# Decay matrices of all eight chunks scanned ahead of the chunks and kept in DRAM

## The chip, the cores and the metric

The kernel runs on one core of a Trainium2 chip. The core has a matrix engine (TensorE, PE in the profile; PEld is its weight load), a vector engine (VectorE, DVE), an engine for activations (ScalarE, ACT), a general one (GpSimd, POOL) and SyncE (SP), whose queue issues every DMA of this kernel. Each engine works through its own instructions in order and waits for semaphores of the others. The metric is the device time of one execution in microseconds (us). Before the change it is 1239.85 us, the median of three runs (1236.53 to 1240.24).

## The reference

One decoder layer in float32: 1024 tokens of width 1024, with 16 learned meta tokens ahead. A normalised input goes through one projection, three groups of heads read it (stick-breaking attention, a Mamba-2 recurrence called SSD, and HGRN2), and their outputs go through an output projection and a squared-ReLU MLP. The change is in the SSD group, which works in chunks of 128 tokens:

```python
acum = jnp.cumsum(a_c, axis=1)
seg = acum[:, :, None, :] - acum[:, None, :, :]
decay = masked_decay(seg, causal[None, :, :, None])          # exp(seg) where s <= t, else 0
cb = jnp.repeat(jnp.einsum('btgn,bsgn->btsg', c_c, b_c), rep, axis=-1)
y_diag = jnp.einsum('btsh,bshp->bthp', cb * decay, x_c)
```

For each chunk and each of 8 heads this needs a 128x128 matrix of decays: the product of the factors exp(a) of all tokens after s up to t. These matrices depend on the step sizes `dt` alone, not on the state that is carried from chunk to chunk.

## The kernel before

**Stages.** The kernel is one long instruction stream per engine. First come the normalised input and its transposes, then the attention with the other projections as fillers between its products, then a short stretch that projects the HGRN2 inputs and computes the meta tokens' states, then eight chunks of 128 tokens (SSD, HGRN2 and the output projection of the chunk before), then the MLP. Matrix products are done with operands split into a high and a low part, three products for one (`split_scaled`, `split`).

**The factors.** `decays()` computes exp(dt * a) for all tokens, transposes it to 8 rows (one per head) and stores it as `dr_g` (8 x 1040). In `chunk(c)` one DMA loads the chunk's 128 factors of all 8 heads, repeated on all 128 partitions, into `dec` (128 x 8 x 128, 512 KB). Two DVE scans (`tensor_tensor_scan` with multiply and add, 128 x 512 each, four heads each) turn it into the decay matrices: the second operand, `ident4`, is four identity matrices, so partition s starts its running product at t = s. The scans stand after the first and the second of seven HGRN2 levels (`LEVELS`, `hg_level`), behind that level's `copy_predicated` on DVE. Levels 3 and 4 multiply `dec` by C·B, and at the chunk's end eight products of `dec` with the inputs give `y_diag`.

**The end of the attention.** The attention's 32 heads (8 query tiles, 4 heads) each need a running product `kp` and a `sg` tile. Between the products of the last heads (`values`, VGAP, SGAP, HGAP) the PE works on fillers (`fill`, `all_fillers`): last of all `z_tile(i)`, i = 1 to 8, called z1 to z8 below. Each z tile is 24 products into one of two `mf` banks; ACT takes the sigmoid of the bank into an `igt` tile, DVE multiplies the bank by it, and a DMA stores the tile to `dr_z`. The bank is free for the next tile but one after the DVE multiply. At the same time `load_wi` loads the eight parts of the next projection's weight by DMA (`st<-in_w_in_dram`) and splits each part on ACT and DVE into `g` tiles. After z8 `ig_all` uses those weights: its first tile, `ig0` (the 16 meta tokens), needs all eight parts.

**What sets the order.** PE's order is that of the code (`queue`, L112). On the other engines the tile framework's scheduler chooses the order from its own estimate, within dependencies and the hints of `behind` (L80). Every queue, SP's too, is then worked through in order: a DMA that waits for a semaphore holds up all DMAs after it. All DMAs of the kernel go through SP's one queue. SBUF tiles come from rings of buffers by tag; `k4` has four buffers (128 x 1072) and serves the attention heads' `kp` and `sg`, then `xb` and `dec` of each chunk. In the profile all vector, scalar and DMA instructions carry the helper's line L96, all products L119 and all transposes L122, so tiles name the work.

Of the kernel before, what the change touches and what calls it, by code (L numbers as in the profile page):

```python
# [13 lines left out]
ALU = mybir.AluOpType  # L14

P = 128
D = 1024
KC = D // P
SEQ = 1024
NT = SEQ // P  # L20
NM = 16
L = SEQ + NM
G3 = L + 16
K4 = L + 48
# [44 lines left out]
def tile_hybrid_block(  # L69
# [8 lines left out]
    fixed, last, lastkv, lastcp, urgent = [False], [None], [None], [None], [None]  # L78

    def behind(i, j):  # L80

        tc.add_manual_dep(i.ins, j.ins.name,
                          mybir.DependencyInfo(mybir.DependencyClass.NoSync, mybir.DependencyReason.DATA),
                          reason="issue order")
# [19 lines left out]
    V, A, G, SY = (Pinned(e) for e in (nc.vector, nc.scalar, nc.gpsimd, nc.sync))  # L104
# [28 lines left out]
    def sb(shape, tag, dt=F32):  # L133
        if tag in ring:
            r = ring[tag]
            r[3] += 1
            at = r[0] + r[3] % r[1] * r[2]
            return cx[:, at:at + shape[0]]
        cnt[0] += 1
        return pool.tile([P] + list(shape), dt, tag=tag, bufs=BUFS[tag], name=f"{tag}_{cnt[0]}")  # L140

    def const(shape, name, dt=F32):
        return pool.tile([P] + list(shape), dt, tag=name, bufs=1, name=name)

    def ps(tag):
        cnt[0] += 1
        return psp.tile([P, 512], F32, tag=tag, bufs=PBUFS[tag], name=f"{tag}_{cnt[0]}")

    def dram(shape, name):
        return drp.tile(list(shape), F32, name=name)  # L150
# [9 lines left out]
    dr_ig = dram([SEQ, 512], "dr_ig")  # L160
    dr_o = dram([SEQ, 256], "dr_o")
    dr_g = dram([8, L], "dr_g")
    dr_h = dram([SEQ, D], "dr_h")
    dr_s = [dram([NQ, P, 512], f"dr_s{i}") for i in range(7)]
    dr_m = dram([NQ, P, 512], "dr_m")
# [96 lines left out]
    ident4 = const([512], "ident4", U8)  # L262
# [519 lines left out]
    dec = decays()  # L782
# [40 lines left out]
    run(dec)  # L823
    attended[0] = True

    KORDER = (4, 5, 6, 7, 0, 1, 2, 3)

    def load_wo(q):
# [6 lines left out]
        if q == 1:  # L835
            for k in KORDER[::2]:
                st = sb([G3], "g3")[:, 0:D].rearrange("p (k n) -> p k n", n=512)
                SY.dma_start(st, w_out[MIXK[k] * P:(MIXK[k] + 2) * P, 512:D].rearrange("(k p) n -> p k n", p=P))
                sts.extend([st[:, 0], st[:, 1]])
            yield  # L840
        for n, k in enumerate(KORDER):
            if q == 0:
# [77 lines left out]
    def hg_level(qb, kx, f4, fp, S, li):  # L920
        b = LEVELS[li]
        n = 64 // b
        kv, qv, sv = (t.rearrange("p q (n t b) -> p q n t b", t=2, b=b) for t in (kx, qb, S))
        fv = f_level(f4, fp, b).rearrange("p q (n t) -> p q n t", t=2)
        pl = ps("pa")
        for p in range(2):
            mm(pl[:, p * P:(p + 1) * P], lhsT=kx[:, p, :], rhs=qv[:, 2 * p:2 * p + 2, :, 1, :], start=True, stop=True)
        lq = V.tensor_tensor(qv[:, :, :, 1, :], qv[:, :, :, 1, :], fv[:, :, :, 0:1].broadcast_to([P, 4, n, b]),
                             op=ALU.mult)
        msk = hmask[:, li:li + 1, :].broadcast_to([P, 4, 64]).rearrange("p q (n b) -> p q n b", b=b)  # L930
        lastcp[0] = V.copy_predicated(sv[:, :, :, 1, :], msk, pl[:, 0:256].rearrange("p (q n b) -> p q n b", q=4, b=b))
        behind(lastcp[0], lq)
        lastkv[0] = G.tensor_tensor(kv[:, :, :, 0, :], kv[:, :, :, 0, :],
                                    fv[:, 0::2, :, 1:2].broadcast_to([P, 2, n, b]), op=ALU.mult)
# [98 lines left out]
    def chunk(c, steps, per):  # L1033

        t0 = (c - 1) * P
        cs = slice(NM + t0, NM + t0 + P)
# [15 lines left out]
        xb = sb([K4], "k4")[:, 0:D].rearrange("p (f t) -> p f t", t=P)  # L1052
        SY.dma_start(xb, dr_x[:, :, cs].rearrange("f p t -> p f t"))
        dec = sb([K4], "k4")[:, 0:D].rearrange("p (h t) -> p h t", t=P)
        SY.dma_start(dec, dr_g[:, cs].rearrange("(o h) t -> o h t", o=1).broadcast_to([P, 8, P]))
        ig = sb([512], "igt")
        SY.dma_start(ig, dr_ig[t0:t0 + P, :])
        zt = sb([512], "a4")
# [10 lines left out]
        for n, b in enumerate(LEVELS):  # L1069
            hg_level(qb, kx, f4, fp, S, n)  # L1070
            if c < 8:
                behind(f_products(hgt[1 - c % 2][1], hgt[1 - c % 2][3], b), lastkv[0])
            if n <= 1:
                dg = dec[:, 4 * n:4 * n + 4, :].rearrange("p h t -> p (h t)")
                behind(V.tensor_tensor_scan(dg, dg, ident4, 0.0, ALU.mult, ALU.add), lastcp[0])
            if n == 0:
                xt = ssd_x(xb, P)
            elif n == 1:
                bt = ssd_b(xb, P)
            elif n == 2:  # L1080
                pc = ps("pb")
                for g in range(2):
                    mm(pc[:, g * P:(g + 1) * P], lhsT=xb[:, 4 + g, :], rhs=xb[:, 6 + g, :], start=True, stop=True)
                py = ps("mq")
                for g in range(2):
                    mm(py[:, g * 256:(g + 1) * 256], lhsT=xb[:, 6 + g, :], rhs=sst[:, g * 256:(g + 1) * 256],
                       start=True, stop=True)
                behind(V.tensor_tensor(y, py.rearrange("p (h d) -> p h d", d=64), inner(cwt[:, c, 0, :], [P, 8, 64]),
                                       op=ALU.mult), lastcp[0])
                behind(G.tensor_tensor(xd, xt, inner(dtt[:, c, :], [P, 8, 64]), op=ALU.mult), lastkv[0])  # L1090
            elif n in (3, 4):
                g = n - 3
                behind(V.tensor_tensor(dec[:, 4 * g:4 * g + 4, :], outer(pc[:, g * P:(g + 1) * P], [P, 4, P]),
                                       dec[:, 4 * g:4 * g + 4, :], op=ALU.mult), lastcp[0])
                if n == 3:
                    behind(G.tensor_tensor(xt, xt, inner(dbc[:, 2, :], [P, 8, 64]), op=ALU.mult), lastkv[0])
                    if nc_:
                        xn = mlp_pre(nc_, ("k4",))
                else:
                    behind(G.tensor_tensor(y, y, xt, op=ALU.add), lastkv[0])  # L1100
            if n == 5:
                behind(G.tensor_tensor(xw, xd, inner(cwt[:, c, 1, :], [P, 8, 64]), op=ALU.mult), lastkv[0])
            elif n == 6:
                behind(G.tensor_tensor(ot, ig[:, 0:256].rearrange("p (h d) -> p h d", d=64),
                                       inner(dtok[:, c - 1].rearrange("p a b -> p (a b)"), [P, 4, 64]),
                                       op=ALU.mult), lastkv[0])
            if n >= 5 and nc_:
                take(steps, 2)
                mlp_tr(nc_, xn, (n - 5,))
                take(steps, per - 2)  # L1110
            else:
                take(steps, per)
# [61 lines left out]
    def out_steps(c):  # L1174
# [5 lines left out]
        for q in range(2):  # L1180
            pp = ps("mf")
            yield from gemm_steps(pp, lambda k, a: mix[:, a, k, :], lambda k, a: wo[q][a][:, k, :],
                                  ks=KORDER)
            V.tensor_tensor(hh[:, q * 512:(q + 1) * 512], pp, hh[:, q * 512:(q + 1) * 512], op=ALU.add)
# [372 lines left out]
    for i, tag in (("s2", "g2"), ("s3", "g2"), ("22", "g1"), ("s1", "g1")):  # L1557
        t = slab(tag)
# [101 lines left out]
```

## Time and profile before

| what | value |
|---|---|
| median of three runs | 1239.85 us |
| the profiled execution's own time | 1240.99 us |
| its span (first to last instruction) | 1239.3 us |
| mean granted TensorE clock | 0.997 |
| busy: PE, DVE, ACT, POOL | 98%, 71%, 47%, 34% of the span |
| end of the attention, z4 to z8 | 334 to 368 us |
| meta states and first HGRN2 inputs | 367 to 389 us |
| chunks 1 to 8 | 390 to about 604 us |
| MLP | from about 600 us to the end |

The rows used below come from these views: the page of the whole execution; the waits of an engine (who it waited for: total us, times, longest); the timeline of an engine (start us, duration us, instruction, and in brackets the idle time ahead of it and what ended it); groups of instructions by line and tile (busy us, mean ns of one); the windows (for a stretch: busy time of PE, PEld, DVE, ACT and POOL, the granted clock, the share of the 16 DMA engines that was busy, GB/s); the chain of waits (start us, us, what); and the DMA issues (KB each and median us from issue to landing). "SPq" is SP's queue, where a row is the issue of a DMA.

### The profile page before, as it was taken

The page shows a single profiled execution, that of the slowest core. Times are in us where ns is not written, and L with a number is a line of the kernel's source. Part 1 is how long each engine was busy: PE and PEld are TensorE (multiplying, and loading weights), DVE is VectorE, ACT ScalarE, POOL GpSimd, SP SyncE. Part 2 cuts the span into 40 slices and gives each one's busy share as a digit, 9 for nine tenths or more (in the row PEclk, how much of TensorE's full clock was granted, in tenths as well). Part 3 has the DMA queues.
Part 4 walks back from the last instruction along what each step waited for, and adds up shares of the span by engine and source line. Part 5 has one row for each costly group of instructions (what it writes and reads, how often), then busy time and mean ns, then how long its engine had stood idle before and what let it go on. Part 6 is the DMA issues. An engine that isn't in the chain of part 4 may idle for free.

```text
span 1239.3 us, 18661 instructions
## 1 busy us (share of the span) xinstructions
PE 1213.2 (98%) x6396; PEld 1040.5 (84%) x6396; DVE 880.3 (71%) x1451; ACT 584.1 (47%) x1237; POOL 425.0 (34%) x498
## 2 busy tenths in 40 slices
PE   8999999999999979999999999999999999999998
PEld 7989999999888868887888888888777888888887
DVE  5777877775333688878456756667998778778777
ACT  6755676664332233233356644454566534344331
POOL 4233222322111457766424646656851000000000
PEclk9999999999999989999999999999999999999999
DMA  6311112233255565562256667677766554554566
GB/s 211 94 41 46 54 39 59 68 94 106 69 137 123 155 220 138 118 121 88 85 158 188 217 210 239 228 237 256 238 213 202 166 161 141 158 156 143 162 198 205
DMA packets 195031, 184.14 MB, mean 149 GB/s; under 512 B 14405, under 2 KB 149853, under 8 KB 194938
## 3 DMA queue, kind: packets, MB, share of 16 engines
q1 hardware_dynamic: 194938, 182.97, 49.4%
q8 instruction: 50, 0.82, 0.3%
q14 instruction: 43, 0.35, 0.1%
HBM read 128.25 MB, written 54.67 MB: 148 GB/s over the span
## 4 chain that ended last, share of the span: by engine, by line
PE 80%; DVE 8%; DMA 3%; issue 3%; POOL 3%; ACT 3%; SPq 1%; DVEq 0%; POOLq 0%; ACTq 0%
PE pa L119 26%; PE mf L119 24%; PE pc L119 17%; PE mq L119 6%; PE pb L119 4%; DVE g L96 2%; DVE k L96 2%; PE pb L122 1%; DVE cx L96 1%; POOL rr L96 1%; DMA g<-in_w_out_dram 1%; DMA g<-in_x_dram 1%; DVE a L96 1%; PE pc L122 1%; POOL cx L96 1%
## 5 line engine op out<-in xcount | busy, mean ns | idle before, releaser
L119 PE MATMUL pa<-g,k 128*128 128x512 f32 x864 | 208.7, 389 | 0.8 <-DVE f L96 0.8
L119 PEld LDWEIGHTS pa<-g,k 128*128 128x128 f32 x864 | 162.0, 188 | 35.2 <-DVE f L96 1.2
L119 PE MATMUL mf<-g,wsA 128*128 128x384 f32 (+2 forms) x624 | 139.2, 358 | 0.0
L119 PE MATMUL mf<-g,wsB 128*128 128x384 f32 (+2 forms) x624 | 137.2, 355 | 0.0
L119 PEld LDWEIGHTS mf<-g,wsA 128*128 128x128 f32 x624 | 104.2, 190 | 6.6 <-DVE g L96 0.3
L119 PEld LDWEIGHTS mf<-g,wsB 128*128 128x128 f32 x624 | 103.4, 189 | 5.8
L119 PE MATMUL mf<-g,g 128*128 128x512 f32 (+1 forms) x408 | 101.1, 395 | 0.0
L96 DVE TENSOR_TENSOR k<-g,k 128x512 fp32r<-128x512 f32 x80 | 80.4, 1006 | 28.1 <-ACT k L96 27.9
L96 ACT CAST g<-cx 128x512 fp32r<-128x512 f32 x80 | 49.5, 619 | 85.8 <-DVE cx L96 59.2
L119 PEld LDWEIGHTS mf<-g,g 128*128 128x128 f32 (+1 forms) x408 | 72.4, 183 | 15.0 <-issue 0.3
L119 PE MATMUL pc<-g,k 128*128 128x512 f32 x336 | 82.5, 389 | 0.0
L96 DVE TENSOR_TENSOR g<-pa,g 128x512 f32<-128x512 f32 (+2 forms) x82 | 54.8, 678 | 36.9 <-PE pa L119 32.3
L96 POOL TENSOR_TENSOR cx<-cx 128x384 f32<-128x384 f32 (+2 forms) x34 | 38.6, 1136 | 118.8 <-ACT cx L96 78.5
L119 PEld LDWEIGHTS pc<-g,k 128*128 128x128 f32 x336 | 63.1, 188 | 13.1
L119 PE MATMUL mf<-g,k 128*128 128x512 f32 x288 | 70.0, 392 | 0.3 <-DVE k L96 0.3
L119 PE MATMUL pa<-g,st 128*128 128x512 f32 x240 | 65.1, 390 | 0.3 <-ACT g L96 0.3
L96 DVE TENSOR_TENSOR g<-cx,g 128x512 fp32r<-128x512 f32 x80 | 60.5, 756 | 4.9 <-ACT g L96 3.5
L119 PEld LDWEIGHTS mf<-g,k 128*128 128x128 f32 x288 | 53.7, 188 | 11.7 <-DVE k L96 0.7
L96 POOL TENSOR_TENSOR g<-g,g 128x512 f32<-128x512 f32 x32 | 45.7, 1438 | 49.8 <-issue 45.5
L96 ACT CAST k<-g 128x512 fp32r<-128x512 f32 x80 | 48.9, 615 | 17.1 <-PE pb L119 9.1
L119 PEld LDWEIGHTS pa<-g,st 128*128 128x128 f32 x240 | 45.0, 188 | 10.1 <-ACT g L96 0.7
L96 DVE SCALAR_TENSOR_TENSOR cx<-cx,cwb 128x384 f32<-128x384 f32 (+1 forms) x72 | 43.4, 603 | 9.2 <-ACT cx L96 8.6
(365 smaller groups left out, 2717.9 us busy)
## 6 DMA issues: line engine op xcount, KB each, us to landing
g<-in_w_up_dram SPq DMA_DIRECT2D x48, 512.0 KB, 4.8
st<-in_w_in_dram SPq DMA_DIRECT2D x51, 256.0 KB, 2.9
cx<-in_w_down_dram SPq DMA_DIRECT2D x48, 256.0 KB, 2.9
wT<-dr_s SPq DMA_DIRECT2D x45, 256.0 KB, 3.0
dr_s<-a SPq DMA_DIRECT2D x40, 256.0 KB, 2.4
g<-in_x_dram SPq DMA_DIRECT2D x16, 512.0 KB, 4.7
dr_s<-st SPq DMA_DIRECT2D x32, 256.0 KB, 2.4
a<-dr_s SPq DMA_DIRECT2D x23, 256.0 KB, 2.8
```

Of the source, the lines that this page charges most:

```text
L96: i = fn(*a, **k)
L119: return queue(nc.tensor.matmul(*a, **k))
L122: return queue(nc.tensor.transpose(*a, **k))
```

## The change

Behind the attention's last head a new loop does for all eight chunks what the chunks did: load the repeated factors into a `k4` tile, scan it twice, and store the result to a new DRAM tensor `dr_d` (8 x 128 x 1024). Each chunk then loads its 512 KB of `dr_d` with one row of 4 KB per partition, where it loaded the factors before, and its two scans are gone.

```diff
     dr_g = dram([8, L], "dr_g")
+    dr_d = dram([NT, P, D], "dr_d")
...
     run(dec)
     attended[0] = True

+    for c in range(NT):
+        dg = sb([K4], "k4")[:, 0:D]
+        cs = slice(NM + c * P, NM + (c + 1) * P)
+        SY.dma_start(dg.rearrange("p (h t) -> p h t", t=P),
+                     dr_g[:, cs].rearrange("(o h) t -> o h t", o=1).broadcast_to([P, 8, P]))
+        for n in range(2):
+            half = dg[:, 512 * n:512 * (n + 1)]
+            V.tensor_tensor_scan(half, half, ident4, 0.0, ALU.mult, ALU.add)
+        SY.dma_start(dr_d[c], dg)
+
...
         dec = sb([K4], "k4")[:, 0:D].rearrange("p (h t) -> p h t", t=P)
-        SY.dma_start(dec, dr_g[:, cs].rearrange("(o h) t -> o h t", o=1).broadcast_to([P, 8, P]))
+        SY.dma_start(dec, dr_d[c - 1].rearrange("p (h t) -> p h t", t=P))
...
-            if n <= 1:
-                dg = dec[:, 4 * n:4 * n + 4, :].rearrange("p h t -> p (h t)")
-                behind(V.tensor_tensor_scan(dg, dg, ident4, 0.0, ALU.mult, ALU.add), lastcp[0])
```

PE's instructions and POOL's stand in the same order as before, ACT's differ in the place of one weight split. SP has 16 DMAs more, and DVE's 16 scans stand at another place. On SP, from the store of z2 on (`dr_z<-igt`, 326.24 us in the trace of before), the order was this. The `k` tiles are `k4` buffers; `qb`, `f` are inputs of HGRN2 levels.

```order
L96 DMA dr_z<-igt_3754 128x512
L96 DMA k_554_4125<-dr_x 128x8x16
L96 DMA qb_4221<-dr_qf 64x2x128
L96 DMA f_555_4128<-dr_f 128x2x16 x2
L96 DMA qb_4221<-dr_qf 64x2x128
L96 DMA dr_z<-igt_3815 128x512
L96 DMA k_575_4248<-dr_x 128x8x128
L96 DMA f_569_4222<-dr_f 128x2x128 x2
L96 DMA st_3971<-in_w_in_dram 128x512
L96 DMA dr_z<-igt_3861 128x512
```

In the changed kernel the same stretch, again from the store of z2, begins like this:

```order
L96 DMA dr_z<-igt_3755 128x512
L96 DMA k_544_4028<-dr_g 128x8x128
L96 DMA dr_d<-k_544_4028 128x1024
L96 DMA qb_4262<-dr_qf 64x2x128
L96 DMA f_563_4169<-dr_f 128x2x16
L96 DMA k_545_4033<-dr_g 128x8x128
L96 DMA f_563_4169<-dr_f 128x2x16
L96 DMA qb_4262<-dr_qf 64x2x128
L96 DMA dr_z<-igt_3816 128x512
L96 DMA k_546_4038<-dr_g 128x8x128
L96 DMA dr_d<-k_545_4033 128x1024
L96 DMA f_577_4263<-dr_f 128x2x128
```

The first load of factors stands where the meta tokens' input stood, its store stands next, and the stores of z3 and z4 and the weight parts come behind loads and stores of the new loop. The end of the loop on SP, down to the last weight part (`st_4099`) and the store of z7 (`igt_4000`), reads:

```order
L96 DMA k_550_4058<-dr_g 128x8x128
L96 DMA st_4085<-in_w_in_dram 128x512
L96 DMA k_551_4063<-dr_g 128x8x128
L96 DMA k_562_4166<-dr_x 128x8x16
L96 DMA dr_z<-igt_3952 128x512
L96 DMA k_583_4289<-dr_x 128x8x128
L96 DMA st_4095<-in_w_in_dram 128x512
L96 DMA dr_d<-k_550_4058 128x1024
L96 DMA dr_d<-k_551_4063 128x1024
L96 DMA st_4099<-in_w_in_dram 128x512
L96 DMA dr_z<-igt_4000 128x512
```

The seventh weight part (`st_4095`) and the eighth stand behind the eighth load, the eighth also behind the last two stores of the loop, and the store of z7 is next. On DVE, from z2's multiply to z4's, the order was:

```order
L96 TENSOR_TENSOR igt_3754<-mf_3704,igt_3754 128x512
L96 SCALAR_TENSOR_TENSOR k_505_3760<-k_505_3760 128x1040
L96 TENSOR_TENSOR igt_3815<-mf_3758,igt_3815 128x512
L96 TENSOR_TENSOR wm_114<-k_506_3761,k_505_3760 128x16
L96 TENSOR_TENSOR k_506_3761<-k_506_3761,k_505_3760 128x1023
L96 SCALAR_TENSOR_TENSOR g_517_3848<-st_3849,nwt,g_516_3847 128x512
L96 TENSOR_TENSOR igt_3861<-mf_3819,igt_3861 128x512
```

It is now (rows with `ident` are the moved scans, printed under the name of their instruction format; the row of 1040 is the last head's running product):

```order
L96 TENSOR_TENSOR igt_3755<-mf_3705,igt_3755 128x512
L96 SCALAR_TENSOR_TENSOR k_544_4028<-k_544_4028,ident_148 128x512 x2
L96 SCALAR_TENSOR_TENSOR k_505_3761<-k_505_3761 128x1040
L96 TENSOR_TENSOR igt_3816<-mf_3759,igt_3816 128x512
L96 TENSOR_TENSOR wm_115<-k_506_3762,k_505_3761 128x16
L96 TENSOR_TENSOR k_506_3762<-k_506_3762,k_505_3761 128x1023
L96 SCALAR_TENSOR_TENSOR k_545_4033<-k_545_4033,ident_148 128x512 x2
L96 SCALAR_TENSOR_TENSOR g_517_3849<-st_3850,nwt,g_516_3848 128x512
L96 SCALAR_TENSOR_TENSOR k_546_4038<-k_546_4038,ident_148 128x512 x2
L96 TENSOR_TENSOR igt_3862<-mf_3820,igt_3862 128x512
```

Three pairs of scans now stand ahead of z4's multiply; one pair more (the fourth) stands ahead of z5's, two more (fifth and sixth) ahead of z6's, and the last two ahead of z7's. The waits in the built program say when buffers are reused: the second load takes the first one's buffer and waits for the first store, the fourth waits for the second store, the sixth for the third, the seventh for the fourth and the eighth for the fifth. As before the change, the sigmoid of each z tile waits for the store of the tile ahead of it.

## The prediction

> **What bounds the kernel now.** I read the page first, then the waits of PE, then the timeline where a wait is long.
>
> ```profile
> span 1239.3 us, 18661 instructions
> PE 1213.2 (98%) x6396; PEld 1040.5 (84%) x6396; DVE 880.3 (71%) x1451; ACT 584.1 (47%) x1237; POOL 425.0 (34%) x498
> ```
>
> PE is busy for 98% of the span, so the whole kernel has 26 us in which PE could be given more to do. A change off PE can win only what PE waits for, and can lose whatever it makes PE wait for. Next, who PE waited for from 425 to 462 us (chunk 2), and then from 462 to 625 us (the chunks after it):
>
> ```profile
> PE pa L119 <- DVE g L96: 5.3, 2, 4.0
> ...
> PE pc L122 <- DVE cx L96: 2.0, 5, 0.4
> PE pa L119 <- POOL cx L96: 0.6, 2, 0.4
> ```
>
> From chunk 3 on there is almost nothing to win: PE waits 0.4 us at each chunk's end for `cx`, the normalised HGRN2 output, whose chain has no scan in it. The one large wait is in chunk 2. The PE timeline there, and DVE's:
>
> ```profile
> 432.49 1.61 PE L119 MATMUL mf<-g,wsA 128*128 128x512 f32 x6
> 438.07 1.19 PE L119 MATMUL pa<-g,cx 128*128 128x128 f32 x4 [3.97 <-DVE g L96]
> 439.05 1.06 PE L119 MATMUL pb<-k 128*128 128x128 f32 x4
> 439.91 1.91 PE L119 MATMUL mq<-sst,k 128*128 128x256 f32 x4
> 441.26 2.92 PE L119 MATMUL mf<-g,wsA 128*128 128x512 f32 x6
> 449.21 0.68 PE L119 MATMUL pa<-g,cx 128*128 128x128 f32 x4 [1.36 <-DVE g L96]
> ...
> 436.50 0.75 DVE L96 SCALAR_TENSOR_TENSOR g<-g,nwt,g 128x512 fp32r<-128x512 f32 x1 [3.77 <-ACT g L96]
> ...
> 425.18 10.55 DMA g<-in_w_out_dram
> ```
>
> DVE stands behind a weight split whose `w_out` data took 10.55 us (last row, chain of waits). PE idles 3.97 us, and then runs slowly: six 512-wide products take 2.92 us where they took 1.61. The windows say why, and what the DMA engines do:
>
> ```profile
> 434.00:436.00 2.00, 0.10 (x1) 0.00 (x0) 0.00 (x0) 0.25 (x1) 0.00 (x0) 1.00 1.04 387
> 440.00:442.00 2.00, 2.00 (x6) 1.59 (x6) 2.00 (x4) 2.00 (x4) 1.72 (x2) 0.50 0.98 329
> ...
> 520.00:522.00 2.00, 2.00 (x12) 1.34 (x10) 1.96 (x4) 0.00 (x0) 2.00 (x4) 1.00 0.97 86
> ```
>
> The granted clock is 0.50 after the idle stretch. The last row is a stretch of chunk 5 in which only a `dr_g` load runs: the DMA engines are 97% busy and move 86 GB/s, where large rows reach 387.
>
> **What a factor load costs.** The DMA issues, then all `dr_g` loads, then a weight part that was issued 2.3 us after a `dr_g` load:
>
> ```profile
> st<-in_w_in_dram SPq DMA_DIRECT2D x51, 256.0 KB, 2.9
> k<-dr_x SPq DMA_DIRECT2D x8, 512.0 KB, 4.5
> k<-dr_g SPq DMA_DIRECT2D x8, 512.0 KB, 8.6
> dr_h<-g SPq DMA_DIRECT2D x8, 512.0 KB, 4.3
> dr_z<-igt SPq DMA_DIRECT2D x8, 256.0 KB, 2.4
> ...
> L96 SPq DMA_DIRECT2D k<-dr_g x8: 359/376/547, 342.4 to 551.8; - x8
> DMA to landing us min/median/max: 7.8/8.6/9.3
> ...
> L96 SPq DMA_DIRECT2D st<-in_w_in_dram x1: 333/333/333, 344.6 to 344.6; - x1
> DMA to landing us min/median/max: 7.4/7.4/7.4
> ```
>
> A `dr_g` load takes 7.8 to 9.3 us each time, twice a `dr_x` load of the same size. The weight part behind it took 7.4 us instead of 2.9: what is issued later queues behind. So a factor load costs 8.6 us alone and, behind another, 512 KB / 86 GB/s = 6.1 us more. A 512 KB store with rows of 4 KB costs 4.3 us to landing (`dr_h`, same shape) and 512 KB / 387 GB/s = 1.4 us of the engines; 256 KB cost 0.7.
>
> **The gain, in the chunks.** Each chunk loses two scans and gets its matrices in 4 KB rows, 1.4 us of the engines instead of 6.1. The 16 scans:
>
> ```profile
> L96 DVE TENSOR_TENSOR_SCAN k<-k,ident 128x512 f32<-128x512 f32 x16 | 20.4, 1272 | 0.0
> ```
>
> These 20.4 us lie on DVE beside PE's work, and by the waits above they are worth nothing from chunk 3 on. In chunk 2 the `dr_g` load for chunk 3 (issued 422.19) lies ahead of `w_out`; with 4.7 us less ahead of it the data lands at about 431.0 instead of 435.73, the split ends near 432.5, and the wait at 434.1 is gone: 3.97 us. With it goes the slow clock: the four groups from 438.07 take 7.08 us, and at full clock 3.7 (six products 1.61, the rest half of what they took): 3.4 us. The wait of 1.36 us at 449 follows a DVE without a break and gets two scans less. Gain 8 us (3.97 + 3.4, and half of 1.36); at least 4, and not above 8.7, as nothing else there waits on it.
>
> **The cost, at the end of the attention.** Here are SP's issues; ACT's sigmoids of z4, z5 and z8 (a sigmoid comes right after its tile's last product, so it marks where PE starts the next tile) with the last weight split; DVE's running product of the last head, z4's multiply, the last split and chunk 1's first use of its matrices; and ig0's products on PE:
>
> ```profile
> 326.24 0.32 SPq L96 DMA_DIRECT2D dr_z<-igt  x1
> 326.65 0.39 SPq L96 DMA_DIRECT2D k<-dr_x  x1
> ...
> 340.63 0.60 ACT L96 ACTIVATE igt<-mf 128x512 f32<-128x512 f32 x1 [2.19 <-PE mf L119]
> 347.53 0.60 ACT L96 ACTIVATE igt<-mf 128x512 f32<-128x512 f32 x1 [4.04 <-PE mf L119]
> 364.68 0.72 ACT L96 ACTIVATE g<-st,nwt 128x512 fp32r<-128x512 f32 x1 [1.49 <-DMA st<-in_w_in_dram]
> 367.43 0.60 ACT L96 ACTIVATE igt<-mf 128x512 f32<-128x512 f32 x1 [2.03 <-PE mf L119]
> ...
> 333.94 2.33 DVE L96 TENSOR_TENSOR_SCAN k<-k 128x1040 f32<-128x1040 f32 x1 [7.73 <-ACT k L96]
> 341.27 0.69 DVE L96 TENSOR_TENSOR igt<-mf,igt 128x512 f32<-128x512 f32 x1 [2.03 <-ACT igt L96]
> 365.44 0.75 DVE L96 SCALAR_TENSOR_TENSOR g<-st,nwt,g 128x512 fp32r<-128x512 f32 x1 [1.20 <-ACT g L96]
> ...
> 404.73 0.68 DVE L96 TENSOR_TENSOR k<-pb,k 128x512 f32<-128x512 f32 x1
> ...
> L119 PE MATMUL mf<-g,g 128*16 128x256 f32 x24 | 3.0, 279 | 0.0
> ```
>
> PE begins z6 at 347.5 and ig0 at 367.4. I follow the new order in this clock. A pair of scans costs 2.5 us.
>
> 1. Load 1 goes out at 326.65, where the meta input went, lands at 335.3; scans to 337.8. Behind them on DVE stand the last head's running product (2.33) and z3's multiply, to 340.8, which z5 can bear (it starts at 340.6). Store 1 waits for the scans, with all of SP behind it, and lands at 342.1.
> 2. Load 2 waits for store 1 and lands at 350.7; z3's store (0.7) and load 3 queue behind it, load 3 landing at 357.5. Scans 3 end at 360.0, z4's multiply at 360.7 instead of 342.0. PE needs z4's bank for z6 at 347.5: **it stands for 13 us**. (Part comes earlier: z4's sigmoid waits for z3's store, 351.4, and a copy for the attention's products is queued behind it on ACT. The end is the same.)
> 3. Store 3 at 360.0, load 4 at 360.4 behind it: 360.4 + 8.6 + 1.4 = 370.4. z4's store (0.7) and load 5 follow: 377.2; a weight part and load 6: 384.0. z5's multiply waits for scans 4: 373.6, and z7 starts then. z5's store lands behind load 6 at 386.1, z6's sigmoid waits for it, and z6's multiply, behind scans 6 and a split, ends at 388.0.
> 4. Store 4 lies behind load 6 too (385.5), so load 7 goes out at 386.6, behind store 6, and lands at 396.6; a weight part and load 8: 403.4. Scans 8 end at 405.9, two splits at 407.4, z7's multiply at 408.1. ig0 starts there: 40.7 us late.
> 5. The last weight part goes out behind store 8 and a split (406.7) and lands at 406.7 + 2.9 + 1.4 = 411.0; ACT 0.72 and DVE 0.75 make it 412.5. ig0's 24 products (3.0 us, or 6 at half clock after the idle stretch) end near 413 instead of 370.4: **42.5 us late**. From ig1 on PE has its banks and weights; chunk 1's matrices are queued at about 407 and, at 404.73 + 42, not due for 40 us.
>
> Eight loads make up most of this: the shift moves by almost eight times any error in one. With 7.8 us a load and a store of 3.1 (2.4 plus 0.7) it is 42.5 - 6.4 - 1.2 = 35; with 9.3 us and scans of 1.6 us each it is 42.5 + 5.6 + 5 = 53. I take 42, near the median rows.
>
> Sum: 1239.3 + 42 - 8 = 1273 of span. The profiled execution took 1240.99, 1.1 above the median, and 1.7 us of it lie outside the span; against the median: 1239.85 + 34 = **1274 us**. The likeliest's own range is 35 - 8 to 53 - 4, that is 1267 to 1289.
>
> Two pages of the Trainium skill bear on this, and nothing above rests on them. "DMA: Bandwidth & Descriptors", "Anatomy of one DMA", gives a fit of 2.0 us plus bytes over 436 GB/s (measured for GpSimd's DMAs): a factor load would cost 3.2 us by it. The eight landings of 7.8 to 9.3 us disagree. "TensorE: Matmul & The Clock Gate", "What's actually happening", says that a window of about 3.4 us without work halves the clock; the 3.97 us idle and the 0.50 behind it agree.
>
> **The rivals.**
>
> *Only the transfers count* (14%). The stores between the loads overlap better than I follow them, and the eight loads run back to back: 335.3 + 7 x 6.1 = 378.0, scans 380.5, last weight part 384.8, split 386.3, against 370.2 when ig0 needs it: 16 us late, minus 8: 1248. For it: the order on SP allows loads 2 and 3 as well as 4, 5 and 6 to be in flight together. Against: loads 2, 4 and 7 wait for a store's landing.
>
> *More is lost behind each stop* (11%). Three stops of over 7 us each bring the clock to 0.50, and each slow group holds up the ACT copy and DVE behind it: 3.4 us three times more, and the gain of chunk 2 gone, since its `w_out` parts queue otherwise: 1274 + 10 + 8 = 1292. Against: while DVE waits for loads, a slower PE costs nothing.
>
> *On the other side: the loads are as cheap as `dr_x`'s* (4% no change or a little faster). If the repeated reads are slow only beside a chunk's traffic, a load costs 4.5 us alone and 1.4 queued. Followed through the same order, z4's multiply ends at 347.8, in time for z6, z7 is 2 us late, ig0 some 6: the end comes to 6 - 8 = -2, 1238. It decides below about 4.7 us a load, since 4.1 us change the end by 36. Against: load, DMA share and GB/s were alike in all eight, one of them (517 to 524) with nothing beside it.
>
> *The fit's cost, as a mechanism here* (3%). Loads of 3.2 us take four waits of 1.3 us out of that order; ig0 is 1 us late and 7 are won: 1233. The rows above speak against it as against the rival before. (This is the skill's fit named above.)
>
> **How the numbers follow.** Forecast 68%, transfers only 14%, more lost 11%, cheap loads 4%, the fit 3%. A measurement of this kernel tells about 0.3% from no change. Slower by more: 68 + 14 + 11 = 93%; within 0.3%: 3 of the cheap loads' 4; faster: 1 + 3 = 4%. The range reaches from between the second case and the first to the third: 1252 to 1292.
>
> **What would show it.** Right: PE idle between 344 and 361 us and again for about 13 us ahead of ig0; the waits of SP name DVE `k`; `w_out` lands in about 6 us in chunk 2, without a wait of 4 us behind it; the MLP's length is the same. Wrong: `dr_g` loads of 5 us or less at the attention's end; z tiles that do not wait; or a stop in the chunks, if they reach their `dr_d` load late.

## The result and the profile after

The changed kernel takes 1259.14 us (median of four runs, 1258.37 to 1259.62) against 1240.04 us before (four runs, 1236.53 to 1240.24): a ratio of 1.0159, with a 95% interval of 1.0147 to 1.0171. It is 19 us slower, where 34 us slower was forecast and 12 to 52 us was the range.

The head of the page of the changed kernel, and the row of the granted clock over 40 slices:

```profile
span 1256.4 us, 18693 instructions
...
PE 1215.9 (97%) x6396; PEld 1043.3 (83%) x6396; DVE 881.0 (70%) x1451; ACT 584.3 (47%) x1237; POOL 419.0 (33%) x498
...
PEclk9999999999978999999999999999999999999999
```

The span grew by 17.1 us, PE's busy time by 2.7: most of the loss is PE standing still. The two slices with digits 7 and 8 (346 to 408 us) are where it stands. Who PE waited for from 310 to 425 us, and then in the first three chunks (425 to 485 us):

```profile
PE pc L119 <- ACT wT L96: 11.3, 3, 5.9
PE mf L119 <- DVE igt L96: 7.5, 1, 7.5
...
PE pa L119 <- DVE g L96: 1.4, 1, 1.4
```

18.8 us of waits at the attention's end that were not there before, and in chunk 2 the wait of 3.97 us is gone. The timeline of PE shows the stops:

```profile
350.12 1.97 PE L119 MATMUL pc<-g,wT 128*128 128x64 f32 x8 [5.88 <-ACT wT L96]
365.26 1.97 PE L119 MATMUL pc<-g,wT 128*128 128x64 f32 x8 [4.58 <-ACT wT L96]
374.35 1.10 PE L119 MATMUL pc<-g,wT 128*128 128x64 f32 x8 [0.85 <-ACT wT L96]
391.89 8.35 PE L119 MATMUL mf<-g,g 128*16 128x256 f32 x40 [7.47 <-DVE igt L96]
```

PE's products stand in the same order in both kernels, so a product's start can be compared one by one; "late" below means its start after minus its start before. The products of the four rows are 6.0, 12.9, 16.9 and 24.7 us late. The four waits make up 18.8 us of that; behind each stop PE also runs slowly for a while (1.97 us for eight small products at 350.12 and 365.26, 1.10 at 374.35). Ig0, the last row, began at 367.2 before; when its products are through, PE is 26.3 us late, 7.5 of them from running slowly. **That is the cost.** Its origin is in the groups of ACT and DVE from 326 to 392 us (idle us just before a group, and what ended it):

```profile
L96 ACT ACTIVATE igt<-mf 128x512 f32<-128x512 f32 x5 | 3.0, 599 | 34.6 <-DMA dr_z<-igt 34.6
...
L96 DVE TENSOR_TENSOR_SCAN k<-k,ident 128x512 f32<-128x512 f32 x16 | 18.7, 1212 | 36.5 <-DMA k<-dr_g 28.7 <-issue 7.9
```

ACT stood 34.6 us ahead of the z tiles' sigmoids, each waiting for the z store before it. All z tiles use one `igt` buffer (the tag has a single one), and each store lay behind factor loads. The copies that PE waits for stand behind those sigmoids. DVE stood 36.5 us ahead of the scans.

**The gain** comes after. The products that were stalled at 438.07 in chunk 2 and that stood at the start of chunk 8 (before, then after):

```profile
586.55 0.71 PE L119 MATMUL pa<-g,cx 128*128 128x128 f32 x4 [0.25 <-POOL cx L96]
```

```profile
460.26 0.61 PE L119 MATMUL pa<-g,cx 128*128 128x128 f32 x4
...
603.70 0.61 PE L119 MATMUL pa<-g,cx 128*128 128x128 f32 x4
```

At 460.26 PE is 22.2 us late, where it was 26.3 us late behind ig0: the stall of 3.97 us is gone. By 445 us (old time) the slow clock behind it is saved too, 19.6 us late. Then PE catches up in steps of 0.4 to 0.8 us, one in each of the chunks that follow, to 17.1 us at 603.70 and 16.7 two microseconds later. So the gain is 6.7 us in chunk 2 and 2.9 us in chunks 3 to 8, together 9.6. The 16.7 us that are left are less than the 19 between the medians mainly because the profiled execution of the kernel before took 1 us more than its median (1240.99 us) and that of the changed kernel 0.8 us less (1258.37).

### The profile page after: what moved, and what is told of

Its sections match the earlier page's. It is cut to its first block, busy times and chain, and to the rows that moved or that the text cites. A ratio compares the mean times of both kernels' runs of the same rounds, so it can differ in the third digit from the quotient of the medians.

```text
span 1256.4 us, 18693 instructions
## 1 busy us (share of the span) xinstructions
PE 1215.9 (97%) x6396; PEld 1043.3 (83%) x6396; DVE 881.0 (70%) x1451; ACT 584.3 (47%) x1237; POOL 419.0 (33%) x498
## 4 chain that ended last, share of the span: by engine, by line
PE 80%; DVE 7%; DMA 5%; issue 3%; ACT 2%; POOL 2%; SPq 0%; DVEq 0%; POOLq 0%; ACTq 0%
PE pa L119 26%; PE mf L119 23%; PE pc L119 17%; PE mq L119 7%; PE pb L119 4%; DVE g L96 2%; DVE k L96 2%; DMA k<-dr_g 1%; PE pb L122 1%; DMA dr_z<-igt 1%; DVE cx L96 1%; PE pa L122 1%; DVE a L96 1%; PE pc L122 1%; POOL ro L96 1%
## 5 line engine op out<-in xcount | busy, mean ns | idle before, releaser
L119 PE MATMUL mf<-g,g 128*128 128x512 f32 (+1 forms) x408 | 105.9, 409 | 7.5 <-DVE igt L96 7.5
L119 PEld LDWEIGHTS mf<-g,g 128*128 128x128 f32 (+1 forms) x408 | 75.4, 191 | 24.1 <-DVE igt L96 7.9
L119 PEld LDWEIGHTS pc<-g,wT 128*128 128x128 f32 x288 | 39.7, 198 | 15.2 <-ACT wT L96 14.1
```

The costliest lines, as they stand in the source:

```text
L119: return queue(nc.tensor.matmul(*a, **k))
```

## The experiments: where the gain comes from

Four kernels were run beside the kernel before on one chip, five rounds each; its median there was 1239.74 us.

**The chunks' side alone.** In the kernel before, the chunks load rows of 4 KB (of the up weight) and do not scan.

```diff
-        SY.dma_start(dec, dr_g[:, cs].rearrange("(o h) t -> o h t", o=1).broadcast_to([P, 8, P]))
+        SY.dma_start(dec, w_up[0:P, 0:D].rearrange("p (h t) -> p h t", t=P))
...
-            if n <= 1:
-                dg = dec[:, 4 * n:4 * n + 4, :].rearrange("p h t -> p (h t)")
-                behind(V.tensor_tensor_scan(dg, dg, ident4, 0.0, ALU.mult, ALU.add), lastcp[0])
```

> Before's kernel with the chunks' side of the change and nothing at the attention's end: each chunk loads 512 KB in rows of 4 KB (from the up weight, so the decay matrices are replaced by weights and the output is another one) and runs no scans. My theory, that the change is a loss of about 26 us ahead of ig0 and a gain of about 9 us in chunk 2: 9 us faster than before, 1231 us, with PE's wait of 3.97 us for the split of w_out at 438 gone. Rival, that PE regains in the chunks only what it lost ahead of them (a delay that the chunks absorb, whatever they load): no gain, 1239 to 1241 us.

Measured: 1230.6 us, ratio 0.9931 (0.9918 to 0.9944), 9.1 us faster. The gain is one of its own and not a regained loss; with the 19 us of the whole change it puts the cost at 28 us.

**Rows alone**: the first edit of the two, with the scans kept.

> The same 4 KB rows, but each chunk keeps its two scans (the decay matrices are again replaced by what the scans make of weights). My theory, that the factor load for chunk 3 holds up w_out in chunk 2: most of the gain, 6 to 7 us, 1233 to 1234 us, and w_out lands in about 6 us. Rival, that the gain comes from DVE's 20 us of scans: 0 to 2 us, 1238 to 1240 us.

Measured: 1235.27 us, 0.9963 (0.9951 to 0.9975), 4.5 us faster, less than the 6 to 7 expected. The timeline of PE says why: the wait of 3.97 us is gone, but with the scans on DVE three small ones are left.

```profile
433.28 0.68 PE L119 MATMUL pa<-g,cx 128*128 128x128 f32 x4 [0.36 <-DVE g L96]
...
439.32 0.68 PE L119 MATMUL pa<-g,cx 128*128 128x128 f32 x4 [0.82 <-DVE g L96]
...
442.85 0.68 PE L119 MATMUL pa<-g,cx 128*128 128x128 f32 x4 [1.47 <-DVE g L96]
```

**Scans alone left out**: the second edit, with the repeated factors loaded as before.

> The chunks load their repeated factors as before, but the two scans are left out (the factors are used where the decay matrices should be). My theory: the 3.97 us wait at 438 stays, the 1.36 us wait at 449 goes, 1 to 3 us faster, 1237 to 1239 us. Rival, that DVE's work is what counts: 6 to 9 us faster, 1231 to 1234 us.

Measured: 1237.51 us, 0.998 (0.997 to 0.9989), 2.2 us faster. The profiled execution was a quick one (1233.85 us): its stop in chunk 2 was 1.79 us instead of 3.97, and the clock was not lowered behind it (1.00 from 436 to 438 us).

```profile
435.53 0.68 PE L119 MATMUL pa<-g,cx 128*128 128x128 f32 x4 [1.79 <-DVE g L96]
```

```profile
436.00:438.00 2.00, 1.55 (x11) 1.28 (x10) 2.00 (x5) 2.00 (x5) 1.64 (x3) 1.00 1.07 395
```

In that trace, and in the one without scans and with rows, PE gains another 2.9 us over chunks 3 to 8; in the two traces that keep the scans (rows alone, and the next one) it gains nothing there. So the scans were worth 3 us in those chunks, mostly at one product group in each (`pa`, at 466.30, 490.52 and so on to 586.55 before), in portions of 0.4 to 0.8 us. The scans and the rows together give 9.1 us where each alone gives 2.2 and 4.5: in chunk 2 either one leaves part of the stall standing.

**Only the order.** The kernel before, complete, with the factor load for chunk 3 issued behind the last load of `w_out`.

```diff
-        SY.dma_start(dec, dr_g[:, cs].rearrange("(o h) t -> o h t", o=1).broadcast_to([P, 8, P]))
+        ld = SY.dma_start(dec, dr_g[:, cs].rearrange("(o h) t -> o h t", o=1).broadcast_to([P, 8, P]))
+        if c == 3:
+            behind(ld, wolast[0])
```

> Before's kernel, whole, with one edit: the factor load for chunk 3 is issued behind the last load of w_out instead of ahead of it. My theory, that chunk 2's stall is only this order on the queue: the wait of 3.97 us and the slow clock behind it go, 6 us faster, about 1234 us, with the scans and the slow loads all still there. Rival, that the transfer is only pushed into another wait (chunk 3 then waits for its factors, or the DMA engines are short either way): within 2 us of 1240 us.

Measured: 1234.63 us, 0.996 (0.9948 to 0.9972), 5.1 us faster. This version leaves nothing out of the computation and beats both kernels. SP's issues and PE's wait:

```profile
423.92 2.30 SPq L96 DMA_DIRECT2D g<-in_w_out_dram  x4
...
429.61 0.64 SPq L96 DMA_DIRECT2D k<-dr_g  x1
```

```profile
433.92 0.68 PE L119 MATMUL pa<-g,cx 128*128 128x128 f32 x4 [0.39 <-DVE g L96]
```

More than half of what the new loop earns is to be had from one line that moves a load by 8 us. The factor load takes 11.2 us to land there, and nobody waits for it.

## The experiments: where the cost comes from

These ran in three rounds each; the kernel before had medians of 1238.91 us (the first four) and 1239.6 us (the others). The ratios are to the kernel before; for a variant of the changed kernel, "no change" is said against the changed kernel's 1259.14 us.

**Quick loads from copies.** The changed kernel, with the factors stored 128 times over, so that each partition reads a copy of its own.

```diff
-        SY.dma_start(dr_g, gz[0:8, 0:L])
+        for j in range(8):
+            SY.dma_start(dr_c[16 * j:16 * j + 16].rearrange("a h t -> h a t"),
+                         gz[0:8, 0:L].rearrange("h (o t) -> h o t", o=1).broadcast_to([8, 16, L]))
...
-        SY.dma_start(dg.rearrange("p (h t) -> p h t", t=P),
-                     dr_g[:, cs].rearrange("(o h) t -> o h t", o=1).broadcast_to([P, 8, P]))
+        SY.dma_start(dg.rearrange("p (h t) -> p h t", t=P), dr_c[:, :, cs])
```

> The changed kernel, whole, but the factors are stored as 128 copies (four MB of stores far ahead of the loop) and the loop's eight loads read distinct rows, one copy for each partition; scans, stores and their order stay. Theory A, that the slow repeated read sets the loop's pace: a load lands in about 4.5 us instead of 8 alone and 1.5 instead of 3.5 to 4.4 behind another; the shift ahead of ig0 falls from 26 us to 6 to 10, with the gain of 9 in the chunks 1238 to 1242 us. Theory B, that the order on SP sets it (stores that wait for scans, loads that wait for a store's landing): 3 of 8 loads stand alone, so some 3 x 3.5 us go at most, 1248 to 1256 us.

Measured: 1311.65 us, 1.0577 (1.0556 to 1.0598). Both theories missed, for a reason that has nothing to do with the loop: the copies' stores stop the whole kernel at their own place, before 165 us and far ahead of the loop.

```profile
PE mq L119 <- DVE f L96: 46.5, 1, 46.5
PE pc L119 <- ACT wT L96: 20.0, 1, 20.0
```

From behind that stop on, the trace can still be read: PE is 70.0 us late ahead of the loop, 79.7 us behind ig0, and 69.9 us at the end of the chunks. The first two loads are there 4.3 and 4.45 us after their issue (396.67 to the scans at 400.96, 406.16 to 410.61), and the loop costs 9.7 us instead of 26.3. That is a hint for theory A, not yet a test.

**Stores on another queue.** The changed kernel, with the loop's stores issued by GpSimd, so that SP never stands behind a store that waits for its scans.

```diff
-        SY.dma_start(dr_d[c], dg)
+        G.dma_start(dr_d[c], dg)
```

> The changed kernel, whole, with one edit: the loop's eight stores are issued by GpSimd instead of SP, so that no load, no z store and no weight part stands behind a store that waits for its scans. Theory B (order on SP): loads 1 to 4 go out one after the other and the later ones as tiles come free, the weight parts are not held up; the shift falls by 10 us or more, to 1249 us or less. Theory A (the repeated reads set the pace): eight loads of 3.5 to 8 us one behind the other take as long as before, 1254 to 1260 us.

Measured: 1259.55 us, 1.0158 (1.0138 to 1.0179): no change. Theory B, the order on SP, would have shown 10 us. But the loads still wait for stores here, through the four `k4` buffers: from 326 to 392 us SP stands 15.8 us, in four waits, for `dr_d<-k`.

**No scans in the loop.** `V.tensor_tensor_scan` is taken out of the loop.

> The changed kernel without the loop's 16 scans (it stores the factors as they are, so the decay matrices are left out of the computation). Loads and stores stay. Theory C, that it is DVE's order that costs (the z tiles' multiplies stand on DVE behind scans that wait for loads): the two waits of 5.9 and 4.6 us for z4's and z5's banks go, the shift falls by 10 to 15 us, 1244 to 1250 us. Theory A or B (loads and the queue): the store still waits for the load's landing and all of SP behind it, only 2.3 us per lone link go, 1252 to 1257 us.

Measured: 1260.74 us, 1.017 (1.0148 to 1.0192): no change, and above what each theory expected. So DVE's order, on which the prediction had hung the z tiles, is not needed for the loss. The edit changed SP's order as well, though: load 3, which went out right behind load 2, now stands behind the second store, and SP waits 29.7 us, seven times, for a load to land.

**Half the loop.** The matrices of chunks 1 to 4 alone; the other chunks load factors and scan.

```diff
-    for c in range(NT):
+    for c in range(4):
```

> The changed kernel, whole, but the loop makes the matrices of chunks 1 to 4 alone; chunks 5 to 8 load their factors and scan them as before the change. My theory, that the shift ahead of ig0 adds up link by link while the gain lies in chunk 2 alone: about half the shift (13 of 26 us) and 7 to 9 us of gain, 1243 to 1247 us. Rival, that four links fit beside the z tiles and only the later ones cost: shift of 6 us or less, 1236 to 1239 us. Rival, that the first waits cost nearly all of it: shift of 18 to 22 us, 1250 to 1254 us.

Measured: 1250.55 us, 1.009 (1.0062 to 1.0118), 11.6 us slower than the kernel before, 4 us above the first theory's range. PE is 16.8 us late behind ig0 (15.8, and 1.0 that its execution was ahead from its first 25 us on), nearly two thirds of the cost for half the loads, and gains 6.8. The time lies in the range of the last rival (the first waits cost nearly all), the shift between the two. The loss is heaviest in the first links: of the four loads three stand alone (1, 2 and 4), of the other four only one (7). And chunks 5 to 8 keep their scans.

**A second buffer for the z tiles**, which otherwise all use one:

```diff
-        zs = sb([512], "igt")
+        zs = sb([512], ("igt", "a3")[i % 2])
```

> The changed kernel, whole, with one edit: the z tiles alternate between two buffers (igt and a3) instead of one, so that a sigmoid no longer waits for the z store before it, which lies behind factor loads. Theory D, that this one buffer turns each late store into a stop of PE: ACT's waits of 10.6, 13.5 and 7.4 us for dr_z go, and the shift ahead of ig0 falls from 26 us to 12 or less, 1246 us or less. Rival E, that DVE's order costs the same alone (z4's and z5's multiplies stand behind scans that wait for loads): the stops only move to the bank that z6 and z7 need, and the shift stays at 22 to 27 us, 1255 to 1260 us.

Measured: 1258.69 us, 1.0157 (1.0142 to 1.0172): no change. Theory D fell: as rival E had it, the stops moved to the banks of z6 and z7.

**Both at once**: the second buffer, and no scans in the loop.

> The same two z buffers, and the loop's 16 scans left out (the decay matrices are left out of the computation), so that neither the store's buffer nor DVE's order can hold PE. Rival E, that each of the two alone is enough for the whole cost: now the shift falls to 12 or less (the weight parts on SP and slow z stores are left), 1235 to 1246 us, though leaving out the scans alone changed nothing. Theory F, that the queue alone (weight parts and loads behind stores that wait) sets ig0's start: 1255 to 1260 us as in all variants so far.

Measured: 1259.8 us, 1.0156 (1.0139 to 1.0173): still no change, so rival E fell too. Theory F's 1255 to 1260 us came true: in this kernel SP waits 28.8 us, seven times, for a load to land before it can issue the store behind it, and the queue as a cause is not excluded. Here are PE's waits from 326 to 400 us, in the order: stores on GpSimd, no scans, second buffer, both.

```profile
PE pc L119 <- ACT wT L96: 15.4, 3, 6.7
PE mf L119 <- DVE igt L96: 4.1, 1, 4.1
```

```profile
PE pc L119 <- ACT wT L96: 15.5, 3, 6.4
PE mf L119 <- ACT g L96: 3.4, 1, 3.4
```

```profile
PE mf L119 <- DVE a L96: 13.6, 2, 10.8
PE mf L119 <- DVE igt L96: 10.0, 2, 8.1
```

```profile
PE pc L119 <- ACT wT L96: 8.1, 1, 8.1
PE mf L119 <- DVE a L96: 6.8, 1, 6.8
PE mf L119 <- ACT g L96: 5.3, 2, 3.2
```

The names change with every edit, and the sum stays between 19 and 24 us. What stays the same as well is the pace of the loads: from the first to the eighth it is 53.1 us in the changed kernel (scans at 334.53 and 387.59) and 53 to 55 us in the four variants, 7.6 to 7.9 us a link (by the scans, or where there are none by the stores that follow the loads), whatever stands between two loads.

**Quick loads without copies.** The changed kernel, with the loop's loads taken as rows of the up weight.

```diff
-        SY.dma_start(dg.rearrange("p (h t) -> p h t", t=P),
-                     dr_g[:, cs].rearrange("(o h) t -> o h t", o=1).broadcast_to([P, 8, P]))
+        SY.dma_start(dg, w_up[0:P, 0:D])
```

> The changed kernel, with the loop's eight loads taken as 4 KB rows of the up weight instead of repeated factors (so the decay matrices are replaced by scans of weights); scans, stores, buffers and every order stay. Theory A, that the slow repeated reads set the pace of it all: loads land in about 4 us, the z stores behind them in 3 to 4 instead of 7 to 8, and the shift ahead of ig0 is 4 to 10 us, with 9 won in the chunks 1234 to 1241 us. Rival B, that the ring of load, scans and store in one queue costs by itself: shift of 15 us or more, 1246 us or more.

Measured: 1239.79 us, 1.0002 (0.9993 to 1.0012): 19 us of the loss are gone with nothing but the loads made quick. PE is 9.2 us late behind ig0 (8.0, and 1.2 that its execution was ahead from its first 25 us on) and wins 9.5 in the chunks. The DMA issues of this kernel (the loop's loads and the z stores), and then windows in the order: before, changed, both edits above at once, this one (busy time of the engines, clock, share of the DMA engines, GB/s):

```profile
k<-in_w_up_dram SPq DMA_DIRECT2D x8, 512.0 KB, 4.6
...
dr_z<-igt SPq DMA_DIRECT2D x8, 256.0 KB, 4.7
```

```profile
342.00:370.00 28.00, 28.00 (x152) 23.19 (x151) 8.75 (x13) 9.02 (x16) 4.26 (x10) 1.00 0.54 136
```

```profile
342.00:390.00 48.00, 31.10 (x128) 24.74 (x126) 20.92 (x22) 7.57 (x14) 6.10 (x14) 0.84 0.86 196
```

```profile
342.00:390.00 48.00, 31.21 (x141) 24.57 (x139) 6.50 (x10) 6.83 (x13) 5.35 (x17) 0.82 0.89 210
```

```profile
342.00:374.00 32.00, 27.11 (x126) 21.94 (x125) 20.46 (x24) 7.12 (x13) 5.77 (x13) 0.89 0.84 280
```

Before, the DMA engines were 54% busy here. Where the loop reads repeated factors they are 84 to 89% busy for 48 us (the changed kernel and the four variants), at 185 to 210 GB/s; with plain rows they move 280 GB/s and the stretch is over in 32 us. The bytes are about the same, 48 x 196 = 9.4 MB in the changed kernel and 32 x 280 = 9.0 MB in this one, but they keep the engines busy for 41 us in the one and for 27 in the other. That would explain why taking away one wait changes nothing: the transfers behind it are still there.

It is not the only reading. In the changed kernel there are seven steps from one pair of scans to the next. The three to loads 2, 4 and 7, which stand behind a store of the loop or wait for its landing, take 37.0 of the 53.1 us, the other four 16.0. With plain rows they take 29.0 and 10.6 of 39.6. So a cheaper load shortens the chain of load, scans, store and next load as well as the engines' time. And no variant took that chain away, as the loads waited for stores through the four `k4` buffers, or the stores for loads on SP. More buffers were not tried, nor all three edits together. What the runs show outright is that the price of the read decides, and that no single one of the three waits does; how much of it acts through the engines' time and how much through the chain stays open.

**Halved loads.** The kernel before, with each of the chunks' factor loads issued in two halves:

```diff
-        SY.dma_start(dec, dr_g[:, cs].rearrange("(o h) t -> o h t", o=1).broadcast_to([P, 8, P]))
+        for j in range(2):
+            SY.dma_start(dec[:, 4 * j:4 * j + 4, :],
+                         dr_g[4 * j:4 * j + 4, cs].rearrange("(o h) t -> o h t", o=1).broadcast_to([P, 4, P]))
```

> Before's kernel, whole, with each factor load of the chunks issued as two halves (four heads each), the same bytes and the same 512 byte pieces. Theory: a repeated load is slow alone (7.8 to 9.3 us) and was quicker behind another one (3.5 to 4.4 us more for the second), so two halves in flight together land in 6 us or less, w_out comes earlier and some of chunk 2's stall goes, 1234 to 1238 us. Rival, that 512 KB in 512 byte pieces just take 6 to 8 us however they are issued: 8 us or more to landing, 1239 to 1241 us.

Measured: 1239.24 us, 0.9995 (0.9986 to 1.0004): no change. The DMA issues show that a half lands in 6.5 us, and the windows of chunk 5, where nothing else runs, what both halves move together:

```profile
k<-dr_g SPq DMA_DIRECT2D x16, 256.0 KB, 6.5
```

```profile
516.00:518.00 2.00, 2.00 (x15) 1.78 (x14) 1.36 (x3) 0.00 (x0) 1.59 (x4) 1.00 0.89 89
518.00:520.00 2.00, 2.00 (x12) 1.43 (x11) 1.87 (x4) 0.00 (x0) 2.00 (x4) 1.00 0.60 71
```

Half the bytes take three quarters of the 8.6 us of a whole load, and the two halves run at 71 to 89 GB/s, as the whole did with 86. The theory that two transfers in flight are quicker fell.

## Why the prediction was right, and where it was not

**The sign and the kind of loss** were right. PE stands still from 344 to 350 and from 361 to 365 us and for 7.5 us ahead of ig0, where the last part of the prediction had 344 to 361 and 13 us; SP waits for DVE `k` (16.0 us, eight times, from 326 to 392 us); `w_out` lands in 6.3 us in chunk 2, and the stall there is gone. The measured 1259 is 15 us below the number. It lies in the range because that reaches down towards the rival of the transfers; it is outside the likeliest's own 1267 to 1289.

**The term that was mis-sized** is the load queued behind another one, taken at 6.1 us, plus 0.7 for a z store or weight part between them. SP's issues and DVE's scans in the changed kernel:

```profile
339.74 0.37 SPq L96 DMA_DIRECT2D k<-dr_g  x1
...
342.27 0.42 SPq L96 DMA_DIRECT2D k<-dr_g  x1
...
354.79 0.38 SPq L96 DMA_DIRECT2D k<-dr_g  x1
...
374.11 0.39 SPq L96 DMA_DIRECT2D k<-dr_g  x1
```

```profile
334.53 2.34 DVE L96 TENSOR_TENSOR_SCAN k<-k,ident 128x512 f32<-128x512 f32 x2 [8.37 <-DMA k<-dr_g]
...
347.90 2.34 DVE L96 TENSOR_TENSOR_SCAN k<-k,ident 128x512 f32<-128x512 f32 x2 [7.02 <-DMA k<-dr_g]
351.99 2.34 DVE L96 TENSOR_TENSOR_SCAN k<-k,ident 128x512 f32<-128x512 f32 x2 [1.11 <-DMA k<-dr_g]
354.25 0.67 DVE L96 TENSOR_TENSOR igt<-mf,igt 128x512 f32<-128x512 f32 x1
363.43 2.34 DVE L96 TENSOR_TENSOR_SCAN k<-k,ident 128x512 f32<-128x512 f32 x2 [7.86 <-issue]
367.85 2.34 DVE L96 TENSOR_TENSOR_SCAN k<-k,ident 128x512 f32<-128x512 f32 x2 [1.49 <-DMA k<-dr_g]
371.33 2.34 DVE L96 TENSOR_TENSOR_SCAN k<-k,ident 128x512 f32<-128x512 f32 x2 [1.14 <-DMA k<-dr_g]
383.54 2.34 DVE L96 TENSOR_TENSOR_SCAN k<-k,ident 128x512 f32<-128x512 f32 x2 [7.84 <-DMA k<-dr_g]
387.59 2.34 DVE L96 TENSOR_TENSOR_SCAN k<-k,ident 128x512 f32<-128x512 f32 x2 [1.71 <-DMA k<-dr_g]
```

Load 2 (issued 339.74) is there at 347.90, 8.2 us; load 4 (354.79) at 363.43, 8.6 (by the start of its scans, for which the view names no releaser); load 7 (374.11) at 383.54, 9.4. These are as the median rows said. Loads 3, 5, 6 and 8 follow their forerunner by 4.1, 4.4, 3.5 and 4.1 us, 16.0 together, where 4 x 6.8 = 27.2 were counted: 11 of the 16 us by which the cost of 42 was too high. The rest is the first store (issued at 336.89, and load 2 goes out behind it at 339.74: 2.8 us instead of 4.3) and smaller differences of the same sort. The rate of 86 GB/s was that of a lone load, and of its fullest two microseconds (520 to 522, the engines 97% busy). In the windows beside it, 518 to 520 and 522 to 524, the engines were 78 and 58% busy, at 94 and 70 GB/s. The shares from 518 to 526 us add up to an estimated 4.8 us of all engines for one load, not 6.1.

**The cause** that the prediction gave, waits strung together by the order on SP and DVE, is where PE stood, but not as it was weighted. The first three stops (5.9, 4.6 and 0.9 us) are those of step 2's parenthesis: the sigmoids of z4, z5 and z6 wait 10.6, 13.5 and 7.4 us for the z store ahead of them, and PE waits for the copy behind each. z4's multiply does stand behind scans 3, at 354.25, but it is done at 354.92, before z6's first product at 355.67: the 13 us for z4's bank, the stop that step 2 rests on, did not come. The last stop of 7.5 us is that of step 4, z7's multiply behind scans 8 and two splits. Taking SP's stores, DVE's scans or the single buffer out of that order changed nothing, while a quick load in the same order took 17 of the 26 us away. So it is the price of the read that decides, in line with the rival "only the transfers count" as far as that goes, though at 26 us and not at its 16: its seven links of 6.1 us left out the waits for stores, and that 4 MB of stores, the z tiles and the weights pass through the same engines; the measured link is 7.6 on average.

**The rival of cheap loads** was worked through to 1238 us, with 4.7 us a load as the point from which it decides. The kernel with loads of 4.6 us took 1239.8: that reckoning came within 2 us, in part because two errors cancel: cost and gain are both over 9 us instead of 6 and 8. The rival of the fit adds up to 1234 (1239.85 + 1 - 7), not 1233; loads of 3.2 us were not run.

**The gain** was put at 8 us and "not above 8.7, as nothing else there waits on it"; it is 9.6. The stall of 3.97 us went as forecast. The slow clock was 2.6 us instead of 3.4: the four groups whose times were added to 7.08 us overlap, and from 438.07 to the end of the last at 444.18 it is 6.1. The wait of 1.36 at 449 stayed (1.4 in the waits of the changed kernel). The step that failed is "worth nothing from chunk 3 on": the scans cost 2.9 us there, as the traces without them show. It was read from waits of 0.4 us at the chunks' ends, whose chain has no scan in it. The row below it in the same view, `POOL cx` with 0.6 us in two waits, was not counted; these are the waits ahead of the `pa` groups at 466.30 and 586.55, and they are gone with the scans, as is the time lost at the same place in chunks 4 to 7, for which the view of the waits has no row.

**More lost behind each stop**: the slow clock did come after each stop, as that rival said (7.5 us in all), but the waits were so much shorter than forecast that the sum stayed below the forecast, and the gain of chunk 2 was not touched.

On the clock, the Trainium skill's "TensorE: Matmul & The Clock Gate", "What's actually happening", has a window of about 3.4 us. The stops of 3.97 and 1.79 us in chunk 2, with granted clocks of 0.50 and 1.00 behind them, agree. In the kernel with halved loads a stop of 3.2 us at the same place was enough (0.50 from 436 to 440 us), a little less than that figure.

## What to carry to other kernels

Before work is moved into another stretch, its transfers should be priced by their time on the DMA engines there, in the state in which they will run, and that time compared with what the stretch has left: here the end of the attention had 46% of its DMA time free, and the eight slow loads took most of it and 20 us more. When a wait is taken away and the time does not move, the waits may be a symptom of something that they share: here the next edit that helped was the one that made the shared load cheaper, not the one that removed the next wait. And a stall behind one late load is first worth a try at the order of issue, which here won 5 us for one line.

## What the runs showed of the hardware

**A load that gives every partition the same rows is slow by itself, not by the size of its pieces.** 512 KB of `dr_x`, also in pieces of 512 bytes but all different, land in 4.5 us and 4 KB rows in 4.6; the repeated factors take 8.6. The copies of the factors, in the same pieces but one copy for each partition, were there after 4.3 us. "DMA: Bandwidth & Descriptors" of the Trainium skill, "Specifications", gives 512 bytes as the smallest piece at line rate: the `dr_x` row, as quick as the 4 KB rows, agrees; the `dr_g` row does not, and the copies show that the difference between them is the repetition.

**Behind another load it adds less than it takes alone**, 3.5 to 4.4 us against 8 to 9, with the DMA engines busy in both cases. The windows of the changed kernel during a lone load (330 to 332 us) and during queued ones (366 to 368, where a store of the loop and a z store run as well):

```profile
330.00:332.00 2.00, 2.00 (x15) 1.87 (x14) 0.00 (x0) 0.35 (x1) 0.00 (x0) 1.00 0.84 95
...
366.00:368.00 2.00, 2.00 (x9) 1.81 (x9) 0.51 (x2) 0.00 (x0) 0.00 (x0) 0.50 1.02 270
```

Part of it is the engines' time that a lone load leaves free (58% busy towards its end, and 4.8 us of all engines in sum, as worked out above). Why the repeated read needs 4.8 us of the engines at all is open. Two halves issued together were not quicker, so it isn't the number of transfers alone.
